# Rows' copies first in mixer one and the dense FFN, S5's copies behind the GDN convolutions, two column blocks' products at the GDN's end

## The chip, the cores and the metric

One core of a Trainium2 chip runs the whole program in one launch. The core has a matrix engine (PE, with PEld for its weight loads), a vector engine (DVE), a scalar engine (ACT), GpSimd (POOL) and a queue engine (SP) that issues most DMA transfers. Each engine works through its own list of instructions in order and waits on semaphores for the others. The metric is the device time of one execution in microseconds; lower is better.

## The reference

Two layers over 256 rows of a residual stream X (256 x 1024, float32). Each layer has three token mixers side by side, between one input and one output projection, and then an FFN: dense in layer 0, a mixture of experts in layer 1.

```python
for layer in range(2):
    hn = rms_norm(x, norm_mix[layer])
    proj = hn @ w_in[layer]                         # 1024 x 3090
    u_s5, z_ssd, xbc_ssd, dt_ssd, qkv_gdn, z_gdn, b_gdn, a_gdn = split(proj)
    y_s5  = s5_mixer(u_s5, ...)                     # complex diagonal scan, GLU, norm; 256 wide
    y_ssd = ssd_mixer(z_ssd, xbc_ssd, dt_ssd, ...)  # conv, chunked scan, gate, norm; 384 wide
    y_gdn = gdn_mixer(qkv_gdn, z_gdn, ...)          # conv, chunked delta rule, norm; 384 wide
    x = x + concat(y_s5, y_ssd, y_gdn) @ w_out[layer]
    hn = rms_norm(x, norm_ffn[layer])
    if layer == 0:
        x = x + (silu(hn @ w_gate) * (hn @ w_up)) @ w_down           # d_ff 3584
    else:
        x = x + moe_ffn(hn, ...)                    # 8 SwiGLU experts of 3584, top 2 of a router
return rms_norm(x, norm_final)

# in gdn_mixer: g = -exp(a_log) * softplus(a_in + dt_bias); inside chunks of 64 a triangular
# system is solved, then a recurrence over chunks gives v_new, o and the state
```

## The kernel before

All matrix products are float32-accurate by splitting: an operand becomes a high part and a remainder, and each product is three matmuls (`mm3`, L221 to L223). Weights come by DMA into a ring of raw tiles (`load`, L198 and L202, issued by SP), and `stage` splits them: `whi` by ACT (L215), `wlo` by DVE or, where it is told so, by GpSimd (L216). PE needs both.

The rows X are transposed by PE (`pthT`, L297) and split by `rows_T` into `hT_hi` (ACT, L302) and `hT_lo` (DVE, L303), 16 blocks of 128x128; every projection needs them. The row statistics of the norm (`sqj` on ACT, `msr` and `xr` on DVE: `rows_rstd`) are applied later, to the products.

In a mixer PE computes the GDN columns (`pqkv`), then those of the SSD (`pxbc`), with convolutions on ACT and DVE (`cacc`, `cth`), then the GDN's pair stage (`LQ`, `DT`, `DM`), the inversion of the triangular blocks in five levels (`pl`, `pd`), and the recurrence (`pw`, `pS`, `pq`, `po`), whose last group is `po1` (L889). Its result goes through `og` and the transposes `ptg` (L854) to `mixg`. The S5 group has a preparation of small operations on GpSimd (`beside[0]` for layer 1: `braw`, `wd`, `rc`, `rs` ...), then the copies `wb` of `wd` (ACT, L451), a main part (L958 to L978 on DVE and GpSimd) and a tail that ends in `m5h` and `m5l`. The output projection sums eight column blocks k in PSUM (`acc`): k 0 and 1 from S5, 2 to 4 from the SSD (`mixs`), 5 to 7 from the GDN (`mixg`); a block has 12 matmuls of 128x512.

The dense FFN runs over 7 blocks of 512 columns in two halves: 48 matmuls each for `pfg` (gate) and `pfu` (up), the gated product `gh`, then `w_down`. The first pair of weights is staged ahead; FF[3] says which engines make its two remainders.

The MoE streams its weights through a ring of 14 slots of 1 MB (`ringa`, `ringb`, L1354 and L1369), whose memory is partly that of the mixer, so the first loads wait for the mixer's last tiles.

A scheduler places the instructions of mixers and FFN on each engine's list from priorities (`PRIO`, `mark`, `high_priority`); the MoE's order on PE is written by hand. `tc.issue_after(i)` makes the scheduler put what is issued under it behind instruction i on the same engine's list; it adds no wait between engines.

Of the kernel before, what the change touches and what calls it, by code (L numbers as in the profile page):

```python
# [8 lines left out]
F32 = mybir.dt.float32  # L9
F32R = mybir.dt.float32r  # L10
# [24 lines left out]
MO = 1  # L35
FF = [1, 1, 1, 1, 2500, 0]
AT = [0, 2, 5]
# [9 lines left out]
def tile_hymba_trunk(ctx: ExitStack, tc: tile.TileContext, p: dict, out: bass.AP):  # L47
# [5 lines left out]
    cur = {}  # L53
# [220 lines left out]
    def along(r, pool):  # L274
# [6 lines left out]
        return rB  # L281

    def rows_T(wcol, pool, scaled=False):

        hh = pool.tile([128, 8, S], F32R, name="hT_hi", tag="hT_hi")
        hl = pool.tile([128, 8, S], F32R, name="hT_lo", tag="hT_lo")
        for n in range(2):
            q = x_rstd(n) if scaled else None
            for f in range(2):
                src = X[:, n, f * 512:f * 512 + 512]  # L290
                if scaled:
                    xn = act.tile([128, 512], F32, name="xn", bufs=3)
                    V.tensor_scalar(out=xn, in0=src, scalar1=q, scalar2=None, op0=OP.mult)
                    src = xn
                pt = ps("G", "pthT")
                for kk in range(4):
                    T.transpose(pt[:, kk * 128:kk * 128 + 128], src[:, kk * 128:kk * 128 + 128], ident)  # L297
                for kk in range(4):
                    k = f * 4 + kk
                    src = pt[:, kk * 128:kk * 128 + 128]  # L300
                    hi, lo = (h[:, k, n * 128:n * 128 + 128] for h in (hh, hl))
                    A.activation(out=hi, in_=src, func=AF.Identity, scale=wcol[:, k:k + 1])  # L302
                    V.scalar_tensor_tensor(out=lo, in0=src, scalar=wcol[:, k:k + 1], in1=hi.bitcast(F32),  # L303
                                           op0=OP.mult, op1=OP.subtract)
        return hh, hl
# [100 lines left out]
    def s5_prep(l, keep, ET, EB, EC, tag="S"):  # L406
# [40 lines left out]
        G.memset(wb, 0.0)  # L447
        for q in range(2):
            for g in range(2):
                r_ = slice(64 * g, 64 * g + 64)  # L450
                A.activation(out=wb[r_, q, :, :, 16 * g:16 * g + 16], in_=wd[r_, q], func=AF.Copy)  # L451
        yield
# [57 lines left out]
    def conv(src, rB, wcols, bias, dst, half=True):  # L510
        if rB is not None:
            V.tensor_tensor(out=dst, in0=src, in1=rB, op=OP.mult)
            src = dst
        acc = act.tile([128, S], F32, name="cacc", tag="cacc", bufs=2)
        if bias is None:
            A.activation(out=acc, in_=src, func=AF.Identity, scale=wcols[3])
        else:
            A.activation(out=acc, in_=src, func=AF.Identity, scale=wcols[3], bias=bias)
        for k in (2, 1, 0):
            sh = 3 - k  # L520
            V.scalar_tensor_tensor(out=acc[:, sh:], in0=src[:, :S - sh], scalar=wcols[k], in1=acc[:, sh:],
                                   op0=OP.mult, op1=OP.add)
        if not half:
            A.activation(out=dst, in_=acc, func=AF.Silu)
            return
        th = act.tile([128, S], F32, name="cth", tag="cth", bufs=2)
        A.activation(out=th, in_=acc, func=AF.Tanh)
        V.scalar_tensor_tensor(out=dst, in0=th, scalar=1.0, in1=acc, op0=OP.add, op1=OP.mult)
# [44 lines left out]
    def layer_mix(l, pm):  # L573
# [55 lines left out]
        for q in range(5):  # L629
# [4 lines left out]
            for c in range(wdth // 128):  # L634
                ch = 2 * q + c
                conv(pp[:, c * 256:c * 256 + 256], rB, gcols(ch), None, qkv_dst[ch], not SIL[l])
        mark('sp', l)

# [17 lines left out]
        if l == 0:  # L656
            A.activation(out=nalog, in_=hp[:, :, 12:24], func=AF.Exp)
            V.tensor_scalar(out=nalog, in0=nalog, scalar1=-1.0, scalar2=None, op0=OP.mult)
        gl = act.tile([128, 2, 12], F32, name="gl")
# [44 lines left out]
        with scope("late", "right"):  # L704
# [183 lines left out]
            for h in range(6):  # L888
                T.matmul(po[:, h * 64:h * 64 + 64], lhsT=LQ[1, h // 3][:, h % 3, 1, :], rhs=vnew[1][:, h, :],  # L889
                         start=True, stop=True)  # L890
            V.tensor_tensor(out=o_g[1], in0=o_g[1], in1=po.rearrange("p (h d) -> p h d", h=6), op=OP.add)
# [253 lines left out]
        for i, k in enumerate(seq):  # L1145
# [11 lines left out]
            else:  # L1157
                continue
            for kk, n, f in order:
                mx = (m5h[:, kk], m5l[:, kk]) if kk < 2 else [(mixs if kk < 5 else mixg)[:, q, (kk - 2) % 3] for q in range(2)]  # L1160
                mm3(accs[n][f], tuple(m[:, n * 128:n * 128 + 128] for m in mx),
                    tuple(w[:, 0, f * 512:f * 512 + 512] for w in staged[kk]), kk == seq[0], kk == seq[7])
        mark('xadd', l)
# [7 lines left out]
    def ffn_dense(hT, pt, beside):  # L1171
        wg, wu, wd = p['ff_w_gate'][0], p['ff_w_up'][0], p['ff_w_down'][0]
        accs = [[ps("PS"[n], f"acc{n}{f}") for f in range(2)] for n in range(2)]
        for m in range(7):
            gh = act.tile([128, 4, S], F32R, name="gh", bufs=2)
            glo = act.tile([128, 4, S], F32R, name="glo", bufs=2)
            for hf in range(2):
# [12 lines left out]
                if m + hf == 0:  # L1190
                    with tc.high_priority(offset=FF[5]):
                        with using(pt):
                            _, r = rows_rstd()
                            rB = along(r, act)
# [9 lines left out]
            if m in beside:  # L1204
                beside[m]()
            w3 = []
# [712 lines left out]
```

## Time and profile before

| | |
|---|---|
| runs of before | 1564.58, 1570.32 and 1572.56 us, median 1570.32 |
| the profiled execution | 1564.13 us, span 1562.4 us |
| mean granted clock of PE, as a share of full speed | 0.98 |
| busy over the span | PE 1476.0 us (94%), DVE 682.3 (44%), ACT 486.4 (31%), POOL 161.0 (10%) |
| stages | mixer of layer 0 to about 229 us, dense FFN to 490, mixer of layer 1 to 678, MoE and the last norm to the end |
| read from HBM | 433.15 MB |

Times in the text are places in the span of the profiled execution. A busy PE is not PE at its peak, since the ends of pipelined matmuls are modelled; idle time of an engine counts only where another has to wait for it.

### The profile page before, as it was taken

The page shows a single profiled execution, that of the slowest core. Times are in us where ns is not written, and L with a number is a line of the kernel's source. Part 1 is how long each engine was busy: PE and PEld are TensorE (multiplying, and loading weights), DVE is VectorE, ACT ScalarE, POOL GpSimd, SP SyncE. Part 2 cuts the span into 40 slices and gives each one's busy share as a digit, 9 for nine tenths or more (in the row PEclk, how much of TensorE's full clock was granted, in tenths as well). Part 3 has the DMA queues.
Part 4 walks back from the last instruction along what each step waited for, and adds up shares of the span by engine and source line. Part 5 has one row for each costly group of instructions (what it writes and reads, how often), then busy time and mean ns, then how long its engine had stood idle before and what let it go on. Part 6 is the DMA issues. An engine that isn't in the chain of part 4 may idle for free.

```text
span 1562.4 us, 23132 instructions
## 1 busy us (share of the span) xinstructions
PE 1476.0 (94%) x9275; PEld 938.5 (60%) x9275; DVE 682.3 (44%) x1350; ACT 486.4 (31%) x821; POOL 161.0 (10%) x281
## 2 busy tenths in 40 slices
PE   4898988999999999989999999999999999999995
PEld 4898968999998998853433344455445443333332
DVE  7888585545556898641010143253324321101112
ACT  4562344354435553322110032243223321001011
POOL 5911073020000010030000000000000000000000
PEclk9999998999999999979999999999999999999998
DMA  6431043555555530098999999999999999999994
GB/s 176 146 109 55 1 127 133 185 166 189 189 163 147 159 104 27 24 401 351 410 411 407 405 407 407 406 402 406 407 402 399 406 412 407 413 412 412 409 404 192
DMA packets 161044, 436.85 MB, mean 280 GB/s; under 512 B 14555, under 2 KB 67892, under 8 KB 146720
## 3 DMA queue, kind: packets, MB, share of 16 engines
q1 hardware_dynamic: 158080, 432.20, 72.9%
q0 software_dynamic: 1072, 2.48, 0.5%
q8 instruction: 75, 1.23, 0.3%
q10 hardware_dynamic: 1776, 0.60, 0.1%
q14 instruction: 41, 0.34, 0.1%
HBM read 433.15 MB, written 2.10 MB: 279 GB/s over the span
## 4 chain that ended last, share of the span: by engine, by line
PE 59%; DMA 5%; DVE 2%; ACT 2%; issue 1%; DVEq 0%; ACTq 0%; SPq 0%
PE pmg L1552 19%; PE macc L1612 10%; PE pmf L1558 5%; PE pmg L1528 5%; PE macc L1537 2%; PE maccf L1618 2%; DMA ringb<-in_moe_w_down_dram 2%; DMA ringa<-in_moe_w_down_dram 2%; PE pmts L1586 2%; DMA ringb<-in_moe_w_up_dram 2%; PE pl L789 1%; PE pd L798 1%; PE pxe L1409 1%; ACT his L1513 1%; PE pmtf L1592 1%
## 5 line engine op out<-in xcount | busy, mean ns | idle before, releaser
L216 DVE TENSOR_TENSOR wlo<-raw,whi 128x1024 fp32r<-128x1024 f32 (+3 forms) x109 | 178.8, 1642 | 103.0 <-ACT whi L215 102.7
L1552 PE MATMUL pmg<-ringb,xs 128*64 128x512 f32 x976 | 220.7, 600 | 0.0
L215 ACT ACTIVATE whi<-raw 128x1024 fp32r<-128x1024 f32 (+3 forms) x110 | 148.2, 1356 | 184.1 <-issue 80.9
L1552 PEld LDWEIGHTS pmg<-ringb,xs 128*64 128x64 f32 x976 | 67.6, 138 | 134.7 <-issue 118.4
L1770 ACT ACTIVATE gs<-pmg,rsl 128x512 f32<-128x512 f32 x49 | 33.7, 688 | 335.8 <-PE pmg L1552 333.9
L1552 PE MATMUL pmg<-ringa,xs 128*64 128x512 f32 x592 | 132.2, 594 | 0.0
L1514 DVE TENSOR_TENSOR los<-ringb,his 128x1024 fp32r<-128x1024 f32 x64 | 75.7, 1222 | 111.1 <-ACT his L1513 110.0
L1612 PE MATMUL macc<-ringb,hs 128*64 128x512 f32 x504 | 113.8, 596 | 1.1 <-DMA ringb<-in_moe_w_down_dram 1.1
L1403 POOL TENSOR_SCALAR od<-iota_f,rkk 128x128 f32<-128x128 f32 x22 | 15.5, 716 | 756.5 <-PE ptoh L1415 756.5
L1552 PEld LDWEIGHTS pmg<-ringa,xs 128*64 128x64 f32 x592 | 41.5, 137 | 83.2 <-issue 76.5
L1612 PEld LDWEIGHTS macc<-ringb,hs 128*64 128x64 f32 x504 | 34.8, 137 | 77.7 <-issue 68.4
L1774 DVE TENSOR_SCALAR gs<-pmf,rsl 128x512 f32<-128x512 f32 x21 | 15.8, 751 | 148.1 <-PE pmf L1558 147.6
L1580 DVE TENSOR_TENSOR hs<-hs,pmts 128x256 f32<-128x256 f32 x49 | 20.0, 416 | 120.1 <-ACT hs L1579 119.3
L221 PE MATMUL pfg<-hT_hi,whi 128*128 128x256 f32 x224 | 63.5, 283 | 9.4 <-DVE xr_t L231 9.4
L1513 ACT ACTIVATE his<-ringb 128x1024 fp32r<-128x1024 f32 x64 | 65.5, 1056 | 21.7 <-PE pmg L1528 17.9
L1612 PE MATMUL macc<-ringa,hs 128*64 128x512 f32 x280 | 63.6, 596 | 1.6 <-DMA ringa<-in_moe_w_down_dram 1.6
L223 PE MATMUL pfu<-hT_hi,wlo 128*128 128x256 f32 x224 | 63.4, 283 | 0.9 <-DVE wlo L216 0.9
L223 PE MATMUL pfg<-hT_hi,wlo 128*128 128x256 f32 x224 | 63.3, 283 | 0.0
L222 PE MATMUL pfg<-hT_lo,whi 128*128 128x256 f32 x224 | 63.2, 282 | 0.0
L221 PE MATMUL pfu<-hT_hi,whi 128*128 128x256 f32 x224 | 63.1, 282 | 0.0
L222 PE MATMUL pfu<-hT_lo,whi 128*128 128x256 f32 x224 | 63.1, 282 | 0.0
L1528 PE MATMUL pmg<-his,xw 128*128 128x512 f32 x224 | 62.9, 403 | 0.3 <-DVE X L1623 0.2
(639 smaller groups left out, 2917.1 us busy)
## 6 DMA issues: line engine op xcount, KB each, us to landing
ringb<-in_moe_w_down_dram SPq DMA_DIRECT2D x74, 1024.0 KB, 12.2
ringb<-in_moe_w_gate_dram SPq DMA_DIRECT2D x142, 512.0 KB, 11.4
ringb<-in_moe_w_up_dram SPq DMA_DIRECT2D x142, 512.0 KB, 11.0
ringa<-in_moe_w_gate_dram SPq DMA_DIRECT2D x82, 512.0 KB, 10.2
ringa<-in_moe_w_up_dram SPq DMA_DIRECT2D x82, 512.0 KB, 10.2
ringa<-in_moe_w_down_dram SPq DMA_DIRECT2D x36, 1024.0 KB, 12.6
raw<-in_w_in_dram SPq DMA_DIRECT2D x16, 1024.0 KB, 6.2
raw<-in_ff_w_gate_dram SPq DMA_DIRECT2D x14, 1024.0 KB, 5.0
```

Of the source, the lines that this page charges most:

```text
L215: A.activation(out=h, in_=src, func=AF.Copy)
L216: on.tensor_tensor(out=l, in0=src, in1=h.bitcast(F32), op=OP.subtract)
L221: T.matmul(o, lhsT=lh, rhs=rh, start=start, stop=False)
L222: T.matmul(o, lhsT=lh, rhs=rl, start=False, stop=False)
L223: T.matmul(o, lhsT=ll, rhs=rh, start=False, stop=stop)
L1513: A.activation(out=h, in_=src, func=AF.Copy)
L1514: V.tensor_tensor(out=l, in0=src, in1=h.bitcast(F32), op=OP.subtract)
L1528: T.matmul(pgu[q], lhsT=xw[:, k, xo:xo + 128], rhs=part[:, kk], start=k == 0 and xo == 0 and part is h, stop=k == 7 and part is l)
L1552: T.matmul(pp[64 * q:64 * q + 64], lhsT=x[:, k, :], rhs=w[q], start=k == 0, stop=k == 7, tile_position=(0, 64 * q), skip_group_check=True)
L1558: T.matmul(pp[32 * j:32 * j + 32], lhsT=x[:, 2 * k2 + j % 2, :], rhs=w[j % 2][j // 2], start=k2 == 0, stop=k2 == 3, tile_position=(0, 32 * ...
L1612: T.matmul(acc[64 * f:64 * f + 64], lhsT=h[:, c, :], rhs=w[:, cc, f * 512:f * 512 + 512], start=m == 0 and c == 0, stop=m == 6 and c == 3, ...
L1770: A.activation(out=g, in_=pgu[i], func=AF.Identity, scale=rs[0])
```

## The change

Four groups of instructions are given another place, and one operation another engine.

1. In layer 0 the GDN's `nalog` (Exp on ACT, scaling on DVE) is put behind the last copies of `rows_T`.
2. In layer 0 the four `wb` copies of S5 (ACT) are put behind the last tanh of the GDN convolutions.
3. In the dense FFN: the remainder of the first `w_up` tile (128x2048) is made by DVE instead of GpSimd (FF[3] from 1 to 0); the row statistics are put behind the rows' copies; GpSimd's S5 preparation for layer 1 is put behind a copy of one element (`begun`) of the first gated product.
4. In layer 1 the products of column blocks 3 and 4 (24 matmuls) are put behind the last matmul of `po1`.

```diff
-FF = [1, 1, 1, 1, 2500, 0]
+FF = [1, 1, 1, 0, 2500, 0]
...
+    @contextmanager
+    def after(*ins):
+
+        with ExitStack() as st:
+            for i in ins:
+                st.enter_context(tc.issue_after(i.ins))
+            yield
+
     def rows_T(wcol, pool, scaled=False):
...
-                    A.activation(out=hi, in_=src, func=AF.Identity, scale=wcol[:, k:k + 1])
-                    V.scalar_tensor_tensor(out=lo, in0=src, scalar=wcol[:, k:k + 1], in1=hi.bitcast(F32),
-                                           op0=OP.mult, op1=OP.subtract)
+                    cur['la'] = A.activation(out=hi, in_=src, func=AF.Identity, scale=wcol[:, k:k + 1])
+                    cur['lv'] = V.scalar_tensor_tensor(out=lo, in0=src, scalar=wcol[:, k:k + 1], in1=hi.bitcast(F32),
+                                                       op0=OP.mult, op1=OP.subtract)
...
-        for q in range(2):
-            for g in range(2):
-                r_ = slice(64 * g, 64 * g + 64)
-                A.activation(out=wb[r_, q, :, :, 16 * g:16 * g + 16], in_=wd[r_, q], func=AF.Copy)
+
+        with after(*[cur['qkv']] * (l == 0)):
+            for q in range(2):
+                for g in range(2):
+                    r_ = slice(64 * g, 64 * g + 64)
+                    A.activation(out=wb[r_, q, :, :, 16 * g:16 * g + 16], in_=wd[r_, q], func=AF.Copy)
...
-        A.activation(out=th, in_=acc, func=AF.Tanh)
+        cur['ct'] = A.activation(out=th, in_=acc, func=AF.Tanh)
...
+        cur['qkv'] = cur['ct']
         mark('sp', l)
...
         if l == 0:
-            A.activation(out=nalog, in_=hp[:, :, 12:24], func=AF.Exp)
-            V.tensor_scalar(out=nalog, in0=nalog, scalar1=-1.0, scalar2=None, op0=OP.mult)
+            with after(cur['la'], cur['lv']):
+                A.activation(out=nalog, in_=hp[:, :, 12:24], func=AF.Exp)
+                V.tensor_scalar(out=nalog, in0=nalog, scalar1=-1.0, scalar2=None, op0=OP.mult)
...
+                cur['po'] = T.matmul(po[:, h * 64:h * 64 + 64], lhsT=LQ[1, h // 3][:, h % 3, 1, :], rhs=vnew[1][:, h, :],
+                                     start=True, stop=True)
...
+            with after(*[cur['po']] * (l == 1 and k in (3, 4))):
+                for kk, n, f in order:
...
-                            _, r = rows_rstd()
+                            with after(cur['la'], cur['lv']):
+                                _, r = rows_rstd()
                             rB = along(r, act)
...
             if m in beside:
-                beside[m]()
+                if m == 0:
+
+                    begun = G.tensor_copy(act.tile([1, 1], F32R, name="begun"), gh[0:1, 0, 0:1])
+                    with after(begun):
+                        beside[m]()
+                else:
+                    beside[m]()
```

What the scheduler makes of it is seen in the order of the instructions. In the rows below, `x4` is a run of four alike; line numbers behind the change are those of the new file (L451 is there L461, L303 is L311, L1354 is L1375).

**ACT in layer 0, near the first `wb`.** Before:

```order
L516 ACTIVATE cacc<-pqkv,half_160 128x256
L527 ACTIVATE cth<-cacc 128x256
L451 ACTIVATE wb<-wd 64x32x16 x2
L215 ACTIVATE whi<-raw 128x1024
L527 ACTIVATE cth<-cacc 128x256
L516 ACTIVATE cacc<-pqkv,half_160 128x256
```

Behind the change:

```order
L215 ACTIVATE whi<-raw 128x1024
L537 ACTIVATE cth<-cacc 128x256
L692 ACTIVATE sqq<-kbq 128x256
L461 ACTIVATE wb<-wd 64x32x16 x4
L692 ACTIVATE sqq<-kbq 128x256 x2
L528 ACTIVATE cacc<-pxbc,half_159 128x256
```

The first two `wb` had 15 splits `whi` ahead of them on ACT, the last two 19; now all four have 22.

**DVE at the step from mixer 0 into the FFN** (`X` is the addition of the products to the rows). Before:

```order
L216 TENSOR_TENSOR wlo<-raw,whi 128x2048
L216 TENSOR_TENSOR wlo<-raw,whi 128x1024
L1167 TENSOR_TENSOR X<-X,acc_2446 128x512
L1167 TENSOR_TENSOR X<-X,acc_2447 128x512
L1167 TENSOR_TENSOR X<-X,acc_2448 128x512
L1167 TENSOR_TENSOR X<-X,acc_2449 128x512
L303 SCALAR_TENSOR_TENSOR hT_lo<-pthT,par_157,hT_hi 128x128 x4
L270 TENSOR_TENSOR msr<-ssr 128x2
L271 TENSOR_SCALAR msr<-msr 128x2
L303 SCALAR_TENSOR_TENSOR hT_lo<-pthT,par_157,hT_hi 128x128
L228 TENSOR_SCALAR xr_y<-msr 128x2
L303 SCALAR_TENSOR_TENSOR hT_lo<-pthT,par_157,hT_hi 128x128
```

Behind the change:

```order
L216 TENSOR_TENSOR wlo<-raw,whi 128x2048
L870 SCALAR_TENSOR_TENSOR mixg<-ptg,half_159,mixg 128x3x128
L1181 TENSOR_TENSOR X<-X,acc_2446 128x512
L216 TENSOR_TENSOR wlo<-raw,whi 128x2048
L1181 TENSOR_TENSOR X<-X,acc_2447 128x512
L1181 TENSOR_TENSOR X<-X,acc_2448 128x512
L1181 TENSOR_TENSOR X<-X,acc_2449 128x512
L311 SCALAR_TENSOR_TENSOR hT_lo<-pthT,par_157,hT_hi 128x128 x16
L270 TENSOR_TENSOR msr<-ssr 128x2
L271 TENSOR_SCALAR msr<-msr 128x2
L228 TENSOR_SCALAR xr_y<-msr 128x2
```

All 16 `hT_lo` stand ahead of `msr`, and a second 128x2048 split stands between the additions.

**PE and SP at the end of mixer 1.** PE before (`acc` are the output products, `pq`, `po`, `pw` the recurrence):

```order
L873 MATMUL pq<-s_6003,kbq 128x64 x6
L882 MATMUL po_6036<-vnew_6001,LQ_5592 128x64 x3
L882 MATMUL po_6036<-vnew_6001,LQ_5607 128x64 x3
L222 MATMUL acc_6854<-wlo,mixs 128x512
L223 MATMUL acc_6854<-whi,mixs 128x512
L222 MATMUL acc_6855<-wlo,mixs 128x512
L223 MATMUL acc_6855<-whi,mixs 128x512
L222 MATMUL acc_6856<-wlo,mixs 128x512
L223 MATMUL acc_6856<-whi,mixs 128x512
L222 MATMUL acc_6857<-wlo,mixs 128x512
L223 MATMUL acc_6857<-whi,mixs 128x512
L828 MATMUL pw<-r_6004,DT_5628 128x64 x3
```

Behind the change:

```order
L877 MATMUL pS<-vnew_6003,kend 64x64 x6
L885 MATMUL pq<-s_6005,kbq 128x64 x6
L894 MATMUL po_6038<-vnew_6003,LQ_5594 128x64 x3
L894 MATMUL po_6038<-vnew_6003,LQ_5609 128x64 x3
L840 MATMUL pw<-r_6006,DT_5630 128x64 x3
L840 MATMUL pw<-r_6006,DT_5645 128x64 x3
L885 MATMUL pq<-s_6005,kbq 128x64 x6
L901 MATMUL po_6066<-vnew_6004,LQ_5624 128x64 x3
L901 MATMUL po_6066<-vnew_6004,LQ_5639 128x64 x3
L221 MATMUL acc_6856<-whi,mixs 128x512
```

The 8 products shown before, and 16 more between `pS` and the first `pq`, have moved behind `po1`; 23 of the 24 stand ahead of `ptg`, which came right behind `po1` before. SP's list at the same place, the first loads of the MoE, before:

```order
L198 DMA raw<-in_w_out_dram 128x2x1024 x4
L1354 DMA ringa_7024<-in_moe_w_gate_dram 128x1024
L1354 DMA ringa_7024<-in_moe_w_up_dram 128x1024
L1354 DMA ringa_7025<-in_moe_w_gate_dram 128x1024
L1354 DMA ringa_7025<-in_moe_w_up_dram 128x1024
L1354 DMA ringa_7026<-in_moe_w_gate_dram 128x1024
L1354 DMA ringa_7026<-in_moe_w_up_dram 128x1024
L1354 DMA ringb_7015<-in_moe_w_gate_dram 128x1024
```

Behind the change:

```order
L198 DMA raw<-in_w_out_dram 128x2x1024 x4
L1375 DMA ringb_7017<-in_moe_w_gate_dram 128x1024
L1375 DMA ringb_7017<-in_moe_w_up_dram 128x1024
L1375 DMA ringb_7018<-in_moe_w_gate_dram 128x1024
L1375 DMA ringb_7018<-in_moe_w_up_dram 128x1024
```

Nine slots of `ringb` now come ahead of all of `ringa`; before, three of `ringa` came first.

## Rows read from the trace of the kernel before

**Rows 1.** By window: PE, PEld, DVE, ACT, POOL busy, clock, DMA share, GB/s.

```profile
0.00:229.00 229.00, 197.00 (x1558) 182.27 (x1559) 182.77 (x511) 104.76 (x219) 95.89 (x174) 0.97 0.34 103
...
678.00:1562.00 884.00, 848.51 (x4485) 357.20 (x4483) 209.23 (x340) 187.60 (x309) 28.85 (x51) 0.98 1.00 395
```

**Rows 2.** Timeline of ACT, PE: start, us, instruction, [idle before <-what ended it].

```profile
21.53 0.22 ACT L657 ACTIVATE nalog<-hp 128x24 f32<-128x24 f32 x1 [6.00 <-DMA hp<-in_gdn_a_log_dram]
...
24.32 0.87 ACT L215 ACTIVATE whi<-raw 128x804 fp32r<-128x804 f32 x1 [0.27 <-DMA raw<-in_w_in_dram]
...
23.08 1.04 PE L221 MATMUL ptok<-whi,hT_hi 128*128 128x402 f32 x2 [4.18 <-ACT whi L215]
```

**Rows 3.** Timeline, ACT and DVE, and a window, near the first `wb`.

```profile
69.24 1.27 ACT L451 ACTIVATE wb<-wd 64x512 f32<-64x512 f32 x2 [5.95 <-POOL wd L311]
...
80.81 1.28 ACT L451 ACTIVATE wb<-wd 64x512 f32<-64x512 f32 x2
...
71.63 1.43 DVE L216 TENSOR_TENSOR wlo<-raw,whi 128x1024 fp32r<-128x1024 f32 x1 [6.27 <-ACT whi L215]
...
70.00:80.00 10.00, 8.36 (x49) 8.36 (x50) 8.34 (x12) 7.85 (x16) 9.93 (x14) 0.66 0.20 49
```

**Rows 4.** A window inside layer 0's pair stage.

```profile
120.00:130.00 10.00, 6.05 (x28) 4.27 (x26) 10.00 (x19) 0.42 (x1) 5.45 (x4) 0.93 0.00 0
```

**Rows 5.** Timeline, PE, end of layer 0's mixer.

```profile
203.84 1.00 PE L889 MATMUL po<-vnew,LQ 128*128 128x64 f32 x8
...
225.45 0.50 PE L222 MATMUL acc<-wlo,mixg 128*128 128x512 f32 x1 [1.13 <-DVE wlo L216]
...
227.17 0.39 PE L223 MATMUL acc<-whi,mixg 128*128 128x512 f32 x1
```

**Rows 6.** Timeline, DVE, POOL, ACT and PE, the step into the FFN.

```profile
219.73 5.67 DVE L216 TENSOR_TENSOR wlo<-raw,whi 128x2048 fp32r<-128x2048 f32 x2 [0.93 <-ACT whi L215]
...
230.70 3.45 DVE L270 TENSOR_TENSOR msr<-ssr 128x2 f32<-128x2 f32 x1 [0.25 <-ACT sqj L268]
...
228.47 4.52 POOL L216 TENSOR_TENSOR wlo<-raw,whi 128x2048 fp32r<-128x2048 f32 x1
...
230.56 1.15 ACT L302 ACTIVATE hT_hi<-pthT,par 128x128 fp32r<-128x128 f32 x4
...
238.83 0.55 PE L221 MATMUL pfg<-hT_hi,whi 128*128 128x256 f32 x1 [9.41 <-DVE xr_t L231]
...
244.72 0.28 PE L221 MATMUL pfg<-hT_hi,whi 128*128 128x256 f32 x1
```

**Rows 7.** A window of the FFN, and the timeline of ACT, DVE and POOL.

```profile
251.00:262.00 11.00, 11.00 (x96) 11.00 (x95) 7.11 (x6) 7.02 (x7) 0.00 (x0) 1.00 0.57 192
...
281.54 1.92 ACT L215 ACTIVATE whi<-raw 128x2048 fp32r<-128x2048 f32 x1 [3.62 <-PE pfg L222]
...
283.49 2.29 DVE L216 TENSOR_TENSOR wlo<-raw,whi 128x2048 fp32r<-128x2048 f32 x1 [1.14 <-ACT whi L215]
...
204.64 0.95 POOL L413 DMA_DIRECT2D braw<-in_s_b_re_dram  x1 [75.54 <-DVE fo_y L228]
...
247.15 0.73 POOL L314 TENSOR_TENSOR rs<-rs,t 128x256 f32<-128x256 f32 x1
```

**Rows 8.** Timeline, PE, end of layer 1's mixer, and a window there.

```profile
660.08 1.55 PE L889 MATMUL po<-vnew,LQ 128*128 128x64 f32 x12
...
665.95 1.74 PE L854 MATMUL ptg<-ident,og 128*128 128x128 f32 x6 [4.32 <-DVE fo_t L232]
...
668.00:670.00 2.00, 2.00 (x6) 1.52 (x5) 0.71 (x2) 0.31 (x1) 0.00 (x0) 0.50 1.02 385
```

**Rows 9.** Timeline, SP's queue, the ring's first loads, and a window behind them.

```profile
660.16 0.34 SPq L1354 DMA_DIRECT2D ringa<-in_moe_w_gate_dram  x1
...
667.83 0.33 SPq L1354 DMA_DIRECT2D ringb<-in_moe_w_gate_dram  x1
...
720.00:740.00 20.00, 20.00 (x122) 5.54 (x122) 0.15 (x1) 1.38 (x2) 0.00 (x0) 1.00 0.79 292
```

More of the change, by code (lines that the diff above doesn't have):

```diff
@@ L888, in layer_mix @@
             for h in range(6):
-                T.matmul(po[:, h * 64:h * 64 + 64], lhsT=LQ[1, h // 3][:, h % 3, 1, :], rhs=vnew[1][:, h, :],
-                         start=True, stop=True)
+                cur['po'] = T.matmul(po[:, h * 64:h * 64 + 64], lhsT=LQ[1, h // 3][:, h % 3, 1, :], rhs=vnew[1][:, h, :],
+                                     start=True, stop=True)
             V.tensor_tensor(out=o_g[1], in0=o_g[1], in1=po.rearrange("p (h d) -> p h d", h=6), op=OP.add)
@@ L1158, in layer_mix @@
                 continue
[L1159 to L1162, printed above, removed]
+            with after(*[cur['po']] * (l == 1 and k in (3, 4))):
+                for kk, n, f in order:
+                    mx = (m5h[:, kk], m5l[:, kk]) if kk < 2 else [(mixs if kk < 5 else mixg)[:, q, (kk - 2) % 3] for q in range(2)]
+                    mm3(accs[n][f], tuple(m[:, n * 128:n * 128 + 128] for m in mx),
+                        tuple(w[:, 0, f * 512:f * 512 + 512] for w in staged[kk]), kk == seq[0], kk == seq[7])
         mark('xadd', l)
```

## The prediction, made before the changed kernel ran

> **What bounds the kernel now.** I read the busy time by stage first [rows 1]. From 678 us on the DMA engines are busy 1.00 of the time: the mixture of experts (MoE) ends when its weights have come, so it moves only with the moment at which that stream starts and with the holes in it. In the first 229 us PE is busy 197 us and DVE 183, neither all the time, so what counts there is what PE or DVE waits for at single places. I then looked for waits of PE and DVE in the order of time and found those the change touches: a wait of PE for the first split weights at the start [rows 2]; a wait of ACT, DVE and PE near 70 us [rows 3]; the end of layer 0's mixer [rows 5]; the step into the dense FFN [rows 6]; the end of layer 1's mixer [rows 8], which hands over to the ring of expert weights [rows 9]. The dense FFN itself is PE-bound: PE is busy 11.00 of 11 us with 96 matmuls, about 0.115 us each, DVE 7.11 [rows 7].
>
> **The sum, part by part.** Times are places in the profiled execution of before, span 1562.4, total 1564.13 us.
>
> *nalog behind the rows' copies.* ACT stood 6.00 us until the parameters `hp` had landed, and only then went on to copies and splits; PE waited 4.18 us for the first `whi` [rows 2]. Now the rest of the copies and three `whi` come ahead of it. The gain has a ceiling: the third `whi` waited for its own load until 24.32 anyway [rows 2], so later PE work can't move by the full 6 us. Bounds 0 (the load decides) and 6.0; the PE wait of 4.18 is nearest. I take 3.
>
> *S5's `wb` copies behind the GDN convolutions.* ACT waited 5.95 us for GpSimd's `wd`; queued behind it was `whi`, behind that DVE's `wlo` (6.27 us of wait) and PE. The stretch 70 to 80 shows the granted clock at 0.66, so PE also ran its first matmuls there at 1.2 GHz [rows 3]. In the new order the four copies stand together, seven splits behind the place of the first two and three behind that of the last two. At that later place ACT had no wait before, at 80.81 [rows 3]; GpSimd's S5 work ahead of `wd` isn't moved, and a place three splits further on, 6.5 us sooner, is about as late. I expect no new wait, or 1 us. What it costs: the four copies (1.27 us per two) now sit in ACT's busier stretch, and all S5 work behind them comes later. Bounds 0 and 7.7 (6.27 and the clock); I take 6.5, near the wait that was seen.
>
> *What S5 being later does.* From 120 to 130 DVE is busy 10.00 of 10 us [rows 4]: there the pair stage is bound by DVE. The ten S5 operations of L958 to L978 move out of it to the first level of the GDN inversion, where they hand over to GpSimd and back four times with DVE's queue behind them. The first relieves, the second delays: GpSimd's four operations in that window are 5.45 us [rows 4], the loss if DVE waits for all of them, and DVE's share of this work is no smaller, the gain if it waits for none. I put the sum at 0, bounds -5 and +5.
>
> *End of layer 0.* Its w_out products now all follow `po1`; before, some stood ahead. `po1` ended at 204.84 and the products at 227.56 [rows 5], 22.7 us; 96 products at 0.246 (seven steps from 225.45 to 227.17, [rows 5]) are 23.6 us. So the tail can't shrink; the gain is the recurrence freed of 12 products (2.9 us), and the wait of 1.13 for a `wlo` that GpSimd's S5 work no longer slows. I take 2.5, bounds 0 and 4.5.
>
> *The step into the FFN.* PE waited 9.41 us before `pfg` [rows 6]. The cause is in DVE's queue: `msr`, an operation on 128x2 elements, took 3.45 us while GpSimd did the 128x2048 `wlo` of 4.52 us, and all `hT_lo` behind it waited. In the new order the 16 `hT_lo` are ahead of the row statistics, and that `wlo` is DVE's. ACT copied four in 1.15 us, 0.29 each [rows 6]. `pfg` first needs four blocks of both row halves, that is 12 copies or 3.5 us, from the end of the products at 227.56 [rows 5] and a first transposition on: it can start near 232 instead of 238.83, 6.8 sooner. The first 28 matmuls took until 244.72, 0.21 each against 0.115 when warm: 2.6 us lost to the half clock. With a wait of 4 us in place of 9.4 I count half, 1.3. DVE's added split (two 128x2048 took 5.67 beside GpSimd, so at most 2.84, [rows 6]) lies between the additions to X while PE still does the last 27 products. If that cover fails, it costs 2.3 to 2.8. Bounds 4 and 11; I take 8.
>
> *GpSimd's S5 preparation in the FFN.* It ran from 204.64 to 247.88 [rows 7], 43 us with the 4.52 `wlo`. It now begins after the first half-block, beside a PE-bound FFN. A split there: `whi` at 281.54 starts when PE lets the buffer go, `wlo` ends at 285.78 [rows 7]; PE's 48 matmuls from the other buffer take to 287.0. The spare time is 1.3 us. A split beside GpSimd took 2.84 instead of 2.29 [rows 6, 7], 0.55 longer, so it fits: cost 0. The Trainium skill (GPSIMD Engine Reference, 8. Key points) says that GpSimd shares its SBUF interfaces with VectorE and contends with instructions of two SBUF inputs, and a split is one. It names no size; by the row of `msr` [rows 6] contention may be a whole GpSimd operation, which I price as a rival below.
>
> *Layer 1's end.* 24 products leave the chain from `pS` to `po1`: at 0.24 that is 5.8 us of PE, partly covering DVE's steps, so 4.6 gained, `po1` ending at 657.0 instead of 661.63. The next wait, 4.32 us for DVE before `ptg` [rows 8], is then filled by 23 products (5.6 us), so `ptg` ends near 663.5 instead of 667.69, and the products behind it run warm, which they didn't (0.50 granted, [rows 8]; about 1.5). PE is thus some 5.7 ahead.
>
> *The ring.* Its first loads were of `ringa`, at 660.16; `ringb` waited until 667.83 for the last `ptg` [rows 8, 9]. Now `ringb` is ahead in SP's queue, so the whole stream starts when `ptg` is done: 663.5, which is 3.3 later. Against that, the window 720 to 740 has a DMA share of 0.79, a hole of 4.2 us [rows 9] where the ring waited for PE to free slots. PE leads by 5.7 + 3.3 = 9 more, so the hole closes. Sum -0.9; bounds -3.5 (`ptg` 2.6 sooner) and +3.5 (`ptg` as before, 7.7 later, less 4.2).
>
> Sum: 3 + 6.5 + 0 + 2.5 + 8 + 0 + 0.9 = 20.9 us, or 1543 against 1564.13. That execution was at the low end of the runs (1564.58 to 1572.56, median 1570.32); against the median it would be 1549. I say **1547**. About 0.5% (7.8 us) is what a measurement of this kernel can tell from no change.
>
> **Rivals.**
>
> 1. *Layer 0's gains are absorbed.* DVE's full stretch [rows 4] takes the 6.5 of `wb`, and the load takes the 3 of the start. For it: DVE is full behind both places. Against: DVE's own wait of 6.27 is part of what goes, and S5's operations leave the full stretch. Left: 2.5 + 8 + 0.9 = 11.4, 1559 against the median. Chance 0.15.
>
> 2. *S5 comes too late.* Its `m5` rows open the w_out sums (k = 0), and with S5's scans moved from ahead of the inversion into it, a late `m5` holds all 96 products. Against: in the order `m5` stands ahead of the last GDN steps, and PE has other work until `po1`. If it came 14 us after `po1`, the sum would be 20.9 - 14 = 7, within the noise: 1563. Chance 0.09.
>
> 3. *GpSimd beside the FFN (slower).* 38 us of preparation span about 7 stages of 5.5 us. If DVE's split is held for a whole GpSimd operation each time, as `msr` was (3.45, [rows 6]), it misses the spare 1.3 by 2.1 us, and if PE's clock then falls to 1.2 GHz, as it had at `pfg`, each stage takes 4.6 more: 7 x 6.7 = 47 us lost, 26 net, 1596. (The Trainium skill's page named above describes this sharing.) It decides for slower from 4.1 us per stage. Against: splits beside GpSimd were 0.55 longer, not 3, and one stage held up doesn't idle PE long. ACT's `wb` there waits on the same `wd`, with `whi` behind it, which would add. Chance 0.06.
>
> 4. *The ring start costs more.* If layer 1's end gains nothing, +3.5 instead of -0.9: a gain of 16.5, 1554. It lies inside my range and is counted with the forecast.
>
> **How the numbers follow.** Forecast 0.70 (gains of 13 to 30 us: 1540 to 1557), rivals 0.15, 0.09, 0.06. The bounds of the single terms add up to a loss of 5 or a gain of 38 if all ended on one side; eight of ten times 1534 to 1562, which takes in rival 1 and part of rival 2. Faster by over 0.5% (below 1562.5): 0.70 + 0.12 of rival 1 = 0.82; within: 0.03 + 0.08 = 0.11; slower: 0.06 and 0.01 of rival 2 at its worst = 0.07.
>
> **What the profile after would show.** If right: no ACT wait at `wb` and none of DVE at the `wlo` behind it; `pfg` waiting under 4 us; PE busy 11 of 11 in the FFN while GpSimd works; `ptg` about 6 us after `po1` with products between; the ring starting with `ringb` after it, and no hole of DMA near the first experts. Wrong would be: a longer inversion with DVE waiting on GpSimd; PE waiting after `po1` for `m5`; `pfg` or `pfu` waiting on `wlo` or `wb`; a stream that starts over 5 us later against `po1` and holes that stay.

## The result, and the profile after

The changed kernel takes 1591.54 us (median of 4 runs, 1591.32 to 1596.34) where the kernel before, run beside it, takes 1570.56 (4 runs, 1564.58 to 1572.56). The ratio is 1.0154, with a 95% interval of 1.013 to 1.0177: slower by 1.5%, where the prediction said 1547, faster. The profiled execution after took 1591.41 us, 27.28 more than that of before (1564.13). One of the experiments below (e7) has executions of two kinds, 32 us apart; both are told of there, because that difference is itself the finding.

The page of after shows where to look. These are two lines of its 40 equal slices (39.7 us each): PE's busy tenths and the clock granted to it.

```profile
PE   4989999999999999999999999999999999999995
PEclk9998569999999999988999999999999999999998
```

PE is busy nine tenths or more in slices 4 to 6 (119 to 238 us), yet its clock there is 8, 5 and 6 tenths. Busy time alone doesn't show the loss, since a matmul at half clock is busy for about twice as long (below, twelve `pl` take 1.50 us and then 2.79).

The windows of after, in 10 us steps (columns: PE, PEld, DVE, ACT, POOL busy with counts, granted clock, DMA share, GB/s):

```profile
130.00:140.00 10.00, 10.00 (x91) 9.94 (x92) 9.63 (x21) 2.94 (x10) 2.50 (x2) 1.00 0.01 2
140.00:150.00 10.00, 7.24 (x42) 6.86 (x39) 9.10 (x14) 1.54 (x5) 2.86 (x2) 0.67 0.01 2
150.00:160.00 10.00, 10.00 (x48) 9.94 (x48) 0.36 (x1) 0.66 (x2) 0.00 (x0) 0.50 0.00 0
...
220.00:230.00 10.00, 9.62 (x74) 9.27 (x73) 6.08 (x28) 4.30 (x12) 0.00 (x0) 0.77 0.01 2
230.00:240.00 10.00, 10.00 (x39) 8.84 (x39) 7.73 (x28) 1.70 (x3) 0.00 (x0) 0.55 0.00 0
```

From 150 to 210 us PE does 46 to 50 matmuls per 10 us at 0.50, that is 1.2 GHz. Near 215 the clock comes back, and from about 226 to 239 it is down again (0.77 and 0.55 in the windows there). Before, the 60 us from 150 to 210 held 507 matmuls at a clock of 1.00. What came just ahead of the first fall is in two timelines of after, PE and DVE (start, us, engine, line, instruction, [idle before <-what ended it]).

```profile
134.44 1.50 PE L798 MATMUL pl<-DM,LQ 128*128 128x64 f32 x12
...
138.03 1.50 PE L807 MATMUL pd<-DT,LD 128*128 128x64 f32 x12
...
144.62 2.79 PE L798 MATMUL pl<-DM,LQ 128*128 128x64 f32 x12 [2.76 <-DVE DM L813]
```

```profile
137.55 2.28 DVE L977 TENSOR_TENSOR_SCAN rb<-m4t,ra 128x512 f32<-128x512 f32 x1 [0.30 <-POOL ra L974]
...
141.96 1.62 DVE L988 TENSOR_TENSOR rb<-rb,rs 128x512 f32<-128x512 f32 x1
...
143.88 0.59 DVE L813 STREAM_TRANSPOSE DM<-DT 128x384 f32<-128x384 f32 x1
...
159.61 0.36 DVE L775 COPY_PREDICATED DT<-lm,pd 128x192 f32<-128x192 uint8 x1 [10.51 <-PE pd L807]
```

The first `pd` of the inversion's first level end near 139.5. DVE should then put them back (L775) and transpose (L813), but S5's scans and products (L977, L988 and more between them) stand ahead in its queue, one of them released by GpSimd's `ra`. So the transposition ends at 144.47 and PE waits 2.76 us. Twelve `pl` took 1.50 us ahead of the wait and take 2.79 behind it. From then on DVE is the one that waits (10.51 us for `pd`): PE at half clock has become the bound, and its clock stays down until about 215, when the inversion is nearly through. What ran just ahead of the rise was a row of small matmuls of S5 (PE's timeline):

```profile
210.84 3.22 PE L1014 MATMUL pyc<-g,ident 128*32 128x128 f32 x26
```

The same places in the trace before, which no group above shows (PE's timeline: first `pd` of the inversion, its last level, and the first `pS` of layer 1; then a window inside the inversion and recurrence):

```profile
144.89 2.17 PE L795 MATMUL pd<-DT,LD 128*128 128x64 f32 x18
...
185.76 0.27 PE L813 MATMUL pd<-DT,LD 64*64 64x64 f32 x1
...
648.78 0.57 PE L865 MATMUL pS<-vnew,kend 128*64 128x64 f32 x12
```

```profile
150.00:210.00 60.00, 59.54 (x507) 55.02 (x507) 40.34 (x123) 20.02 (x57) 5.36 (x7) 1.00 0.03 7
```

And the rows of after that answer to the groups (timelines of ACT, PE and SP's queue, then two windows, one beside GpSimd's work in the FFN and one behind the ring's start):

```profile
22.73 1.64 ACT L215 ACTIVATE whi<-raw 128x804 fp32r<-128x804 f32 x2 [4.30 <-DMA raw<-in_w_in_dram]
...
81.67 2.55 ACT L461 ACTIVATE wb<-wd 64x512 f32<-64x512 f32 x4
...
216.14 0.27 PE L825 MATMUL pd<-DT,LD 64*64 64x64 f32 x1
...
262.69 0.39 PE L223 MATMUL acc<-whi,mixg 128*128 128x512 f32 x1
...
267.38 0.35 PE L221 MATMUL pfg<-hT_hi,whi 128*128 128x256 f32 x1 [2.54 <-DVE hT_lo L311]
...
673.88 0.57 PE L877 MATMUL pS<-vnew,kend 128*64 128x64 f32 x12
...
682.39 2.82 PE L901 MATMUL po<-vnew,LQ 128*128 128x64 f32 x12
...
693.07 0.49 PE L866 MATMUL ptg<-ident,og 128*128 128x128 f32 x3
...
693.69 0.34 SPq L1375 DMA_DIRECT2D ringb<-in_moe_w_gate_dram  x1
```

```profile
290.00:310.00 20.00, 20.00 (x126) 17.88 (x125) 10.95 (x7) 9.44 (x8) 20.00 (x33) 1.00 0.81 240
...
750.00:770.00 20.00, 20.00 (x116) 5.59 (x114) 1.50 (x2) 1.37 (x2) 0.00 (x0) 1.00 1.03 410
```

Going from place to place, before to after, gives the balance. First `pd`: 144.89 to 138.03, 6.9 sooner. From there to the 64x64 level: 40.9 us to 78.1, 37.2 lost. From that level to the last product (227.56 [rows 5] to 263.08): 41.8 to 46.9, 5.1 lost. From the last product to `pfg` (238.83 [rows 6]): 11.3 to 4.3, 7.0 gained. From `pfg` to the end of the span (1562.4 to 1589.6): 1323.6 to 1322.2, 1.4 gained. Sum: 27.2 us slower. PE has done about the same work at each of these places in both traces, DVE has not: at the first `pd` some 7 us of S5's operations, which were done by then before, still stand in its queue.

### The profile page after: what moved, and what is told of

Its sections match the earlier page's. It is cut to its first block, busy times and chain, and to the rows that moved or that the text cites. A ratio compares the mean times of both kernels' runs of the same rounds, so it can differ in the third digit from the quotient of the medians.

```text
span 1589.6 us, 23127 instructions
## 1 busy us (share of the span) xinstructions
PE 1512.8 (95%) x9275; PEld 970.4 (61%) x9275; DVE 684.6 (43%) x1351; ACT 486.0 (31%) x821; POOL 169.1 (11%) x281
## 4 chain that ended last, share of the span: by engine, by line
PE 48%; DMA 15%; DVE 2%; ACT 1%; issue 1%; DVEq 0%; SPq 0%; ACTq 0%
PE pmg L1573 14%; PE macc L1633 7%; DMA ringb<-in_moe_w_up_dram 6%; DMA ringa<-in_moe_w_up_dram 4%; PE pmg L1549 4%; PE pmf L1579 4%; DMA ringb<-in_moe_w_down_dram 3%; PE macc L1558 2%; DMA ringa<-in_moe_w_down_dram 2%; PE maccf L1639 2%; PE pmts L1607 1%; PE pl L801 1%; PE pd L810 1%; PE pxe L1430 1%; ACT his L1534 1%
## 5 line engine op out<-in xcount | busy, mean ns | idle before, releaser
L1573 PEld LDWEIGHTS pmg<-ringa,xs 128*64 128x64 f32 x592 | 41.9, 137 | 83.3 <-issue 78.1
## 6 DMA issues: line engine op xcount, KB each, us to landing
ringa<-in_moe_w_gate_dram SPq DMA_DIRECT2D x82, 512.0 KB, 10.7
```

The source lines that it names most:

```text
L1573: T.matmul(pp[64 * q:64 * q + 64], lhsT=x[:, k, :], rhs=w[q], start=k == 0, stop=k == 7, tile_position=(0, 64 * q), skip_group_check=True)
```

## The experiments

**Theory A:** the wait that S5's moved operations make for PE in the inversion's first level drops its clock to 1.2 GHz, and the inversion's small matmuls then don't raise it; the loss is the clock's. **Rivals:** B (the expectations also call it B'), the loss is S5's lateness or the longer queues as such, and the clock only shows it; M, the clock fell because of which matmuls the move left between the inversion's own, not because of the wait.

**e1_no_wb** undoes the `wb` move alone.

```
-        with after(*[cur['qkv']] * (l == 0)):
+        with after():
```

> The changed kernel with S5's wb copies left to the scheduler in layer 0 as before (parts 1, 3 and 4 kept). Theory A: PE's clock is the cause. With S5's main part back ahead of the inversion, no wait of 2.8 us stands at the inversion's first level, the inversion runs at a granted clock of 1.00 and takes 41 us from its first to its last pd as before, not 78; the time is that of before less about 1 (nalog) and 9.4 (the step into the FFN: 6.8 and the half clock of 2.6), plus about 2 for layer 1's end: 1562. Theory B, GpSimd's S5 preparation beside the FFN or the new end of layer 1 cost the time: it stays above 1580.

1555.17 us (1553.64 to 1557.29; before in the same job 1568.62), ratio 0.9924 (0.9898 to 0.995): faster than before. With S5 back at its place the inversion keeps its clock (e1's window 150 to 160, then PE's timeline):

```profile
150.00:160.00 10.00, 10.00 (x90) 9.38 (x89) 6.52 (x15) 4.01 (x12) 0.00 (x0) 1.00 0.00 0
```

```profile
144.57 2.17 PE L807 MATMUL pd<-DT,LD 128*128 128x64 f32 x18
...
203.52 1.00 PE L901 MATMUL po<-vnew,LQ 128*128 128x64 f32 x8
...
230.35 0.40 PE L221 MATMUL pfg<-hT_hi,whi 128*128 128x256 f32 x1 [2.66 <-DVE hT_lo L311]
```

**e2_only_wb** is that move alone, on the kernel before: the other conditions emptied in the same way, `begun` left out, and

```
-FF = [1, 1, 1, 0, 2500, 0]
+FF = [1, 1, 1, 1, 2500, 0]
```

> The kernel before with part 2 alone (wb copies behind the GDN convolutions). Theory A: the inversion falls to half clock as in the changed kernel and the layer-0 mixer ends some 36 us later; nothing else is gained: 1600 to 1607, slower than the changed kernel. Theory B (parts 3 or 4 are to blame): about before, or 5 us faster, since a wait of 6 us is gone: 1565.

1601.17 us (1594.36 to 1609.71), ratio 1.0208 (1.0152 to 1.0264). Its four executions took 1594.36, 1594.44, 1607.89 and 1609.71; the traced one is 1607.89. The same wait of 2.76 us for `DM` stands in its trace (PE's timeline), and the same half clock behind it, which lasts longer there, to about 244 us. So e1 and e2 put the whole loss on this one part; they don't tell A from B or M.

```profile
141.88 2.79 PE L798 MATMUL pl<-DM,LQ 128*128 128x64 f32 x12 [2.76 <-DVE DM L813]
```

**e3_warm** adds 24 useless matmuls to the changed kernel, six per unit in the inversion's second level (`wf` is a constant 128x128 tile in fp32r, the type of the split operands).

```
                     pl = ps("G", "pl")
+                    if l == 0 and b == 4:
+                        for _ in range(6):
+                            T.matmul(pl.rearrange("p (k c) -> p k c", k=4), lhsT=wf, rhs=wf.unsqueeze(1).to_broadcast([128, 4, 128]), start=True, stop=True)
```

> The changed kernel with 24 useless matmuls of 128x512 (fp32r, results overwritten) added in the inversion's second level of layer 0: more work for PE. Theory A: they raise the granted clock back to 1.00 for the levels behind them, which saves about half of some 50 us, less 6 to 10 us for the matmuls themselves: 1572 to 1578. Theory B', the inversion is longer because DVE waits in S5's chain or because PE has more to do there: the 24 matmuls come on top, 1597 to 1602.

1580.88 us (1578.85 to 1583.35), ratio 1.0094 (1.0068 to 1.012): more work, 10.7 us less time than the change. The clock holds through the inversion (it falls behind it, from about 191), but the scheduler's order moved too: S5's tail now stands behind `po`, and PE waits for it there (windows, then PE's timeline):

```profile
150.00:160.00 10.00, 10.00 (x84) 9.67 (x84) 3.82 (x9) 2.33 (x8) 0.00 (x0) 1.00 0.00 0
...
210.00:220.00 10.00, 3.09 (x15) 2.37 (x13) 6.45 (x14) 1.81 (x3) 4.26 (x2) 0.74 0.00 0
```

```profile
217.34 1.87 PE L1043 MATMUL pn<-ones,rc 128*128 128x1 f32 x8 [5.43 <-ACT rc L1039]
```

That is the prediction's rival 2, which the change itself doesn't show: there the first product (236.90) follows `po` at once. The run missed the 1572 to 1578 of A because of it, and it changed two things, so the next four separate them.

**e5_stall** starts from e1, where the clock held and S5 is at its old place, and puts one useless DVE operation of 3.3 us ahead of one unit's transposition (`idle` is a tile of 128x24). **e6_stall2** is the same with 48 in place of 24, 6.5 us.

```
                     put(u, b, halves(pd, b) if HB[l] else half(heads(pd), b, 1))
+                    if l == 0 and b == 2 and u == units[2]:
+                        V.tensor_reduce(out=idle, in_=DT[u][:, 0, :].unsqueeze(1).to_broadcast([128, 24, 128]), op=OP.add, axis=AX.X)
```

> The wb move is undone (as in e1: the row copies, the S5 copies of layer 0 at their old place), and one useless VectorE sum over 24 x 128 numbers, some 3 us, is put into the first level of layer 0's inversion, ahead of one unit's transposition. S5's operations stay where they were before. Theory A (a wait of TensorE of some 2 to 3 us in the inversion's first level drops its clock for the rest of the inversion): the inversion runs at a granted clock of 0.50 and the time is 1580 to 1592. Rival M (not the wait, but what the move left between the inversion's small matmuls, without the 128x384 ones of e1, drops the clock): 1555 to 1560, the stall costs its own 2 to 3 us at most.

> As e5, with a sum of 48 x 128, some 6.5 us. Theory A: 1583 to 1597, clock 0.50 in the inversion. Rival M: 1558 to 1563, the stall's own length on top of e1.

e5: 1583.47 us (1579.21 to 1589.79; before in this job 1568.09), ratio 1.0121 (1.0079 to 1.0164), 28 us above e1. e6: 1589.72 (1584.98 to 1598.55), ratio 1.0161 (1.0111 to 1.021), 35 us above e1. In e5 (PE's timeline, then a window):

```profile
142.97 2.17 PE L808 MATMUL pd<-DT,LD 128*128 128x64 f32 x18
...
151.02 0.88 PE L799 MATMUL pl<-DM,LQ 128*128 128x64 f32 x6 [1.03 <-DVE DM L816]
152.43 0.46 PE L1084 MATMUL p<-up_inc,gl 128*128 128x128 f32 x2 [0.53 <-DVE xD L1073]
...
155.01 4.05 PE L808 MATMUL pd<-DT,LD 128*128 128x64 f32 x18
```

```profile
150.00:160.00 10.00, 8.46 (x45) 8.26 (x45) 7.82 (x16) 2.69 (x7) 0.00 (x0) 0.66 0.01 2
...
220.00:230.00 10.00, 10.00 (x59) 9.70 (x59) 8.14 (x43) 1.23 (x3) 0.00 (x0) 0.57 0.00 0
```

Two waits of PE, 1.03 and 0.53 us, cost 28 us. Eighteen `pd` took 2.17 us before them and take 4.05 behind. S5 is at its old place here and PE's order up to the stall is that of e1, so in the inversion a wait alone is enough to drop the clock: M falls there, and with it B as a cause of the fall. A wait is not always needed: in the same trace the clock falls again in the recurrence (0.57 from 220 to 230) with PE busy 10.00 of 10 and no wait of it over 0.2 us since 152. There M stands, and no run tests it.

**e7_fill_first** and **e8_fill_late** put 8 of the same useless matmuls into the changed kernel, with S5's tail at its place: e7 at unit 0 of the first level, ahead of the wait, as shown; e8 with `b == 8 and u == units[3]`, in the third level, behind it.

```
+                    if l == 0 and b == 2 and u == units[0]:
+                        for _ in range(8):
+                            T.matmul(pl.rearrange("p (k c) -> p k c", k=4), lhsT=wf, rhs=wf.unsqueeze(1).to_broadcast([128, 4, 128]), start=True, stop=True)
```

> The changed kernel with 8 useless 128x512 fp32r matmuls (some 2 us) ahead of the first level of the inversion in layer 0, so that TensorE comes to the wait for VectorE some 2 us later; S5's tail stays ahead of the last po as in the change. Theory A: the wait of 2.76 us shrinks to under 1 us, the inversion runs at 1.00, the time is 1555 to 1568. If the clock falls all the same: 1592 to 1595.

> The changed kernel with 8 of the same useless matmuls in the third level of the inversion (b = 8), some 30 us behind the wait. If a stretch of such matmuls brings the clock back: granted clock 1.00 from about 175 us on, the time 1570 to 1580. If the clock stays down as long as the inversion's own small matmuls last: 1591 to 1596.

e7: of eleven executions six took 1558.15 to 1567.79 us (mean clock 0.974 to 0.980; against before 0.9974, interval 0.995 to 0.9997), five 1593.77 to 1596.56 (0.956 to 0.960). It is one program with one order; the two medians, 1562.2 and 1594.3, differ by 32.1 us. The profiled execution is of the second kind; that the first kind kept its clock in the inversion is not traced. The mean clocks say so: by an estimate from them, (1 - 0.956) x 1592.5 = 70 us of the profiled execution went to half clock, and (1 - 0.977) x 1560.6 = 36 us of one of 1562.38. In the profiled one the wait had shrunk to 1.42 us, and the clock fell all the same (PE; twelve `pl` take 2.77 us again):

```profile
144.86 0.43 PE L1002 MATMUL py<-SI,cm 128*128 128x64 f32 x2 [1.42 <-DVE SI L995]
...
147.70 2.77 PE L803 MATMUL pl<-DM,LQ 128*128 128x64 f32 x12
```

e8: 1578.18 us (1574.06 to 1585.77), ratio 1.0075 (1.0048 to 1.0101), 13 us below the change. The wait of 2.76 us stands and the clock falls; at the eight matmuls it comes back and stays until the recurrence, where it falls again (0.50 from 210 to 220; PE, then a window of e8, from its slowest execution, 1585.77):

```profile
172.00 3.42 PE L800 MATMUL pl<-wf 128*128 128x512 f32 x8
```

```profile
180.00:190.00 10.00, 10.00 (x98) 9.72 (x97) 7.08 (x14) 3.80 (x11) 0.00 (x0) 1.00 0.01 2
```

So 3.4 us of work that computes nothing earned 13, and the small matmuls, under which the clock had stayed down for some 27 us, kept it once it was up.

**e11_fill_wait** puts those 8 matmuls at unit 0 of the second level (`b == 4`), the place of the wait itself.

> The changed kernel with 8 useless 128x512 fp32r matmuls ahead of the inversion's second level, at the very place of the wait of 2.76 us, which they fill for some 2 us; S5's last rows come just behind the last po. If the clock then holds in every execution, this is the change at full clock with 2 us of filler. If the wb move is then worth its predicted 6.5: 1555.2 - 6.5 + 2, some 1551 (1548 to 1553). If S5's later place in the inversion costs what wb gained, or more: 1557 to 1566, with waits of PE in the inversion or behind po for S5. If the clock falls all the same: 1590 and above.

1562.7 us (1556.42 to 1566.55, 10 runs; before in this job 1567.31), ratio 0.9966 (0.9944 to 0.9989). Of the wait 0.37 and 0.22 us are left on the two sides of the filler, the clock is 1.00 through the inversion, and in no execution did the time jump. But the result lies 7.5 us above e1 (5.4 without the 2.1 of filler), so even with the inversion at full clock the `wb` move gains nothing and seems to lose (the two ratios' intervals still overlap). Where, PE's timeline of e11 shows (its slowest execution, 1566.55):

```profile
196.81 2.82 PE L906 MATMUL po<-vnew,LQ 128*128 128x64 f32 x12
...
201.72 0.87 PE L871 MATMUL ptg<-ident,og 128*128 128x128 f32 x3 [1.13 <-DVE og L868]
...
203.29 0.63 PE L224 MATMUL acc<-wlo,m5h 128*128 128x512 f32 x1
...
226.38 0.50 PE L225 MATMUL acc<-whi,mixg 128*128 128x512 f32 x1 [2.40 <-DVE mixg L875]
...
236.04 0.36 PE L223 MATMUL pfg<-hT_hi,whi 128*128 128x256 f32 x1 [2.82 <-DVE hT_lo L313]
```

All 96 w_out products now come behind `po`. PE has nothing to cover its waits for `og` and `mixg` with, and the clock falls in the recurrence (0.82 and 0.67 in the windows 190 to 200 and 200 to 210), so the first eight products run at 0.43 us each (203.29 to 203.72) instead of 0.23. From the end of `po` (199.63) to `pfg` it takes 36.4 us; in e1 a dozen products stand ahead of that end (204.52) and `pfg` follows 25.8 us behind it.

**e4_no_end** is the change without the part on layer 1's output products; **e9_no_wb_end** leaves out both that and the `wb` move; **e10_only_ffn** leaves out `nalog`'s place as well, so that only the step into the FFN remains.

```
-            with after(*[cur['po']] * (l == 1 and k in (3, 4))):
+            with after():
...
-            with after(cur['la'], cur['lv']):
+            with after():
                 A.activation(out=nalog, in_=hp[:, :, 12:24], func=AF.Exp)
```

The first pair of lines is in all three, the second in e10 alone.

> The changed kernel without part 4 (products of column blocks 3 and 4 left among the recurrence of layer 1). If part 4 costs what the trace shows (from pS to the end 2 us more than before): 1589. If it gains the 0.9 that was predicted: 1592.

> Parts 1 and 3 alone (nalog's operations and the sums of squares behind the row copies, GpSimd's S5 preparation behind the gate), the S5 copies of layer 0 and layer 1's output products as before. If the end of layer 1 is worth nothing, as the change without it showed: 1555, the same as e1 within 2. By the prediction's term for layer 1's end (0.9 gained): 1556; by rival 4 (that end costs 7): 1548.

> Part 3 alone (the step into the FFN: sums of squares behind the row copies, GpSimd's S5 preparation behind the gate). By the prediction's term (8, bounds 4 to 11) on the before of the same job: ratio 0.995 (0.993 to 0.9975). If all that e1 gained over before (13.4) is this step's: ratio 0.9915. The rest of e1's gain would then be nalog's place at the start, 3 by the prediction, 1 by the trace of the change.

e4: 1591.49 us (1590.11 to 1595.67) against the change's 1591.54. e9: 1555.13 (1554.33 to 1556.73), ratio 0.9936 (0.9916 to 0.9956), against e1's 1555.17. Against their own kernel before, e9 and e1 are at 0.9936 and 0.9924. So layer 1's end is worth nothing to within some 2 us, with the rest of the change or without it. e10: 1555.95 (1555.41 to 1556.95; before 1565.57), ratio 0.994 (0.992 to 0.9959): the step into the FFN alone gives 9.6 us, and `nalog` 0.8 on top of it. Both, and e1, beat the kernel before and the change.

## Why the prediction was wrong

**The step that failed is "What S5 being later does", put at 0 with bounds of -5 and +5.** Its mechanism was there: it said that S5's operations would hand over to GpSimd and back with DVE's queue behind them, in the first level of the inversion, and the wait of 2.76 us for `DM` is just that, inside the bounds. What it left out is what such a wait does to PE. It priced a wait at its own length; here 2.76 us of waiting were followed by a clock of 0.50 from about 144 to 215 us, nearly the whole inversion, and 37.2 us were lost. Shown: one program's executions differ by 32.1 us (e7); a stall without S5 makes the fall (e5, e6); filling the wait stops it (e11). The prediction had priced the half clock at `pfg` (2.6 us), at `wb`, at layer 1's end and in rival 3, but not behind a new wait in the inversion. It didn't ask what kind of work stands there. The kernel before held a sample: beside the window of [rows 4] PE waited 1.53, 1.10, 0.74 and 0.77 us between 123 and 130 us, and the clock fell too, but 128x384 matmuls `ptok` came next and by 136 it was back (PE's timeline and a window of before):

```profile
130.18 0.66 PE L221 MATMUL ptok<-whi,hT_hi 128*128 128x384 f32 x1 [0.77 <-DVE cacc L521]
```

```profile
130.00:140.00 10.00, 9.82 (x49) 9.45 (x50) 9.96 (x23) 4.08 (x6) 0.00 (x0) 0.73 0.29 100
```

In the change all `ptok` are done by 121 us, ahead of the wait, and nothing of their size follows it in the inversion.

**`wb` behind the convolutions (6.5).** The waits went as it said: ACT copies at 81.67 without a wait, and the first `pd` comes 6.5 us sooner than in e1 (138.03 against 144.57). But that is not the old wait carried through. On DVE the change leads e1 by 6.3 us at the last `kT`, by 0.8 at `rk_y` (DVE's timeline, of after and then of e1), and at the first `pd` PE is 6.5 ahead with some 7 us of S5's operations on DVE put off, the relief that the term on S5 had named:

```profile
72.26 1.25 DVE L538 SCALAR_TENSOR_TENSOR kT<-cth,cacc 128x256 f32<-128x256 f32 x1
...
97.24 0.17 DVE L228 TENSOR_SCALAR rk_y<-aqk 128x24 int32<-128x24 int32 x1
```

```profile
78.94 0.83 DVE L538 SCALAR_TENSOR_TENSOR kT<-cth,cacc 128x256 f32<-128x256 f32 x1
...
98.01 0.17 DVE L228 TENSOR_SCALAR rk_y<-aqk 128x24 int32<-128x24 int32 x1
```

That the number came out as forecast is luck; how much of it belongs to `wb` and how much to S5's leaving DVE's full stretch, no run separates.

**End of layer 0 (2.5)** has the wrong sign: in the change it lost 5.1 (the balance above). The clock alone can make that: in the windows 220 to 240 it stood at half for some 14 us, by an estimate from their 0.77 and 0.55, and half of these, 7 us, are lost. In e11, at full clock in the inversion, the stretch from `po` to `pfg` takes 10.6 us longer than in e1, more than the 6.5. The step counted products as a load that the recurrence would be freed of. In e1 they covered its waits, and the clock stayed at 1.00 there. How much of this is S5's tail, which is a little later in e11 than in the change, no run separates.

**The step into the FFN (8)** was right: the wait is 2.54 instead of 9.41 [rows 6], 7.0 us sooner on the balance, and 9.6 as a change of its own (e10). It is the only part with a gain that can be measured.

**`nalog` (3)** was 0.8 (e10 to e9, hardly apart from nothing), inside its bounds of 0 and 6 but mis-sized: ACT now waits 4.30 us for `raw` instead, and the two `whi` behind that wait start at 22.73, where before they started at 22.16. The load that the prediction had named as the ceiling for the third `whi` holds these as well.

**GpSimd beside the FFN (0, rival 3)** was right: with POOL busy 20.00 of 20 us, PE is busy 20.00 at a clock of 1.00.

**Layer 1's end and the ring (0.9)** came to 0 within some 2 us (e4, e9). The pieces differ from the forecast: without products between its steps the last recurrence fell to half clock (12 `po` in 2.82 us instead of 1.55 [rows 8]), so `ptg` ended 19.7 us behind the start of `pS` (673.88 to 693.56), where before it was 18.9 (648.78 to 667.69), not sooner, and the ring started with it. Against that, the hole of [rows 9] did close (DMA share 1.03 from 750 to 770). That the sum came out near the forecast is luck: the first piece was wrong, and that the two cancel is read from the traces, not tested.

Rival 1 came in part: the load took most of `nalog`'s 3, and in DVE's queue the lead that `wb` gave had shrunk to 0.8 at `rk_y`. Rival 3 did not appear; that its 1596 lies near the measured time is chance. Rival 2 came only in e3, where the clock was held and the order moved. Of the signs named for a wrong forecast, "a longer inversion with DVE waiting on GpSimd" is the one that came, but the length is the clock's, not GpSimd's.

## What to carry to other kernels

Before moving work into a stretch of small fp32 matmuls, look at what DVE and GpSimd then do between two of its levels: a wait of one to three microseconds there cost some thirty here, because it was paid in PE's clock for the next 50 to 100 us. Read the granted clock and the number of matmuls per window beside the busy share; a PE that is busy 10.00 of 10 may be doing half the work. And products that stand ahead of a chain are not only its load: ask which waits they cover before moving them behind it.

## What was unexpected about the hardware

PE's records show it busy 61.00 of 61 us from 149 to 210 in the change, and the clock stayed at 0.50 throughout:

```profile
149.00:210.00 61.00, 61.00 (x286) 59.81 (x286) 20.28 (x43) 8.08 (x25) 0.00 (x0) 0.50 0.00 1
```

The inversion's matmuls (128x64 fp32) kept a clock of 1.00 in the kernel before (150 to 210), in e1, and in e8 from 180 to 200. So this work went on at either level and did not raise the clock in those 61 us; with eight fp32r matmuls of 128x512 it rose (e8). What else does is not settled: in the change it rose behind the 26 `pyc`, and in e2 the same 26, at 208.10, left it at 0.50 until about 244. The Trainium skill (TensorE: Matmul & The Clock Gate, Part 1) says that the gate follows how busy PE has recently been; by the profile's busy time alone these traces disagree with that, since the same busy share stands at both clocks. What the gate counts in these matmuls, no run here shows. Whether a wait of about 1.4 us drops the clock seems not to be fixed either: in e7 the same program took the longer time in five of eleven executions.
